# Smaller step intervals for the long convolution (CVL 900 to 760) and for the scan strands (SLG 1.0 to 0.85) in the two hybrid layers of a long fp32 kernel

## The chip, the cores and the metric

The kernel runs on one core of a Trainium2 chip. The metric is the device time of one execution in microseconds. Three executions of the kernel before gave 3419.37, 3421.62 and 3433.52 us; the median, 3421.62 us, is the time that a changed kernel is held against. A further execution was profiled.

## The reference

A model of four layers works on 512 tokens of width 1024 (and in its first two layers on 256 context tokens besides), all in fp32. The first two layers are of another kind and the change does not reach them. The last two are "hybrid" layers, which compute, cut to what matters:

```
proj = h @ w_in                                   # split into q,k,v, z_a, gates of the scan, cf_val, cf_glu, z_b, gate_lg
qkv  = silu(depthwise_conv_centred(qkv, qkv_conv_w))
o    = gated_delta_chunked(q, k, v, g, beta)      # forward, and once more backward in time, 4 heads
y_a  = (rms(o) * dn_norm_w * silu(z_a)) @ w_dn_out
u    = cf_val * sigmoid(cf_glu)                   # 512 channels x 512 tokens
u    = depthwise_conv_centred(u, cf_conv_w) + cf_conv_b      # 31 taps
u    = silu(layer_norm(u, cf_ln_w, cf_ln_b))
y_b  = (u * silu(z_b)) @ w_cf_out
y    = (gate0 * y_a + gate1 * y_b) @ w_out
```

`gated_delta_chunked` takes, for each head and direction, the inverse of a triangular 64x64 matrix per chunk of 64 tokens, and then walks the 8 chunks in order with a state of 128x128.

## The kernel before

**Products.** Each fp32 product is made of three matmuls for each 128 rows of the contraction: activation and weight are split into a high and a low part, and H·wh (L344), L·wh (L347) and H·wl (L348) are summed in PSUM. A product of a full 1024-row contraction is so 8 times 3 = 24 matmuls of 128x512, one with w_cf_out 12. Everything else that TensorE does in a hybrid layer is small: transposes, the inverses and the scans.

**Strands.** `hybrid` (run twice, called hybrid 0 and 1 below) writes its products in this order: gates of the scan, projections of heads 0 and 1, `cf_proj` (8 products, which give the four 128-channel tiles of u), projections of heads 2 and 3, 16 gate products, 4 z_b products ("zb"), then `cf_norm` (the layer norm of the convolution's output), and `branch(1, Yb)`, 8 products of 12 matmuls. Beside them run generators ("strands"): `head(0)`, which does the inverse and scan of head 0 and then of head 2, `head(1)` with heads 1 and 3, and `cf_conv`, the 31-tap convolution, tile by tile: centre tap on ScalarE (L1788), 20 taps on VectorE (L1794, names `cfa<-ld,vecs,cfa`), 10 taps on GpSimd in pairs of a multiply and an add (L1962, L1963), and a VectorE add that joins the two sums (L1967).

**What sets the order.** A planner keeps a clock `now`. After each three matmuls of a product `mmacc` calls `tick`, which adds their planned time and then writes each strand's next step if it is due. A step that yields `(a, b)` adds `a` to the clock and makes the strand due again after `b` x 2.5 x `slow`. Each convolution tap yields `(0, CVL)`, each part of a scan step or of an inverse its own pair, such as `(220, 750)`; `slow` is SLG for both head strands and 1.0 for the convolution. The first TensorE instruction of each step is pinned behind the one that stands ahead of it, so the order on TensorE between products and steps is the planner's. On the other engines a scheduler places the instructions. Where the program needs a strand's end, it calls `wait`, which moves the clock to the earliest due time and writes the steps due then, of all strands, with no product between them. After the last zb product stand these lines:

```
    while any(s[1] is conv for s in K.back):
        K.wait()
    Yb = cf_norm(K, l, zb, U)
```

**cf_norm.** VectorE sums the four tiles, TensorE sums over channels with ones (L1982), the mean is broadcast by a matmul (L388) and subtracted (L1988), the mean square is made in the same way (L374, L364, GpSimd's power L366, L388), and each tile is scaled (L1992), put through Silu (L1993), multiplied with its zb tile (L1994) and split into high and low parts (L324, L325). The first branch product waits for these parts.

**A scan step.** TensorE multiplies with the state (L2124), VectorE makes Pb (L2127), TensorE multiplies with the inverse (L2133), VectorE and ScalarE scale (L2137, L2138), TensorE makes the state's update (L2145), VectorE the state (L2151), TensorE the output (L2157, L2160). An **inverse** is five rounds of a 32-matmul group on a mask of GpSimd's (L739, mask L731), a VectorE transpose (L742) and a ScalarE copy (L743), a second 32-matmul group (L748) and a VectorE subtraction (L749), on which the next L739 waits. L2087, L2088, L2089, L2102 and L2103 prepare it on VectorE.

Of the kernel before, what the change touches and what calls it, by code (L numbers as in the profile page):

```python
# [1756 lines left out]
        K.free(xc[j]["l"], sz[j])  # L1757
    K.free(*ht)

CVL = 900  # L1760
SLG = 1.0
PT = range(1, 31, 3)
HP = 10

# [16 lines left out]
def conv_n(K, dst, src, n, taps, bias=None, skip=()):  # L1781
# [7 lines left out]
    for j in range(len(taps)):  # L1789
# [4 lines left out]
        nc.vector.scalar_tensor_tensor(dst[:, a:b], src[:, a + o:b + o], taps[j], dst[:, a:b], MUL, ADD)  # L1794
        yield 0, CVL


def hybrid(K, CH, l, X):
# [59 lines left out]
    def proj(h):  # L1858
        pre[h] = gdn_proj(K, l, h, X, w)

    def head(a):
        pads = CH.pads(K.p2)
        for h in (a, a + 2):
            while h not in pre:
                yield 0, 2000
            yield from gdn_head(K, CH, l, h, *pre.pop(h), gcT, ngT, beT, bkT, eglT, gcd, egd, Ya, pads)
        K.free(*pads)
# [7 lines left out]
    for h in range(2):  # L1875
        proj(h)
        K.background(heads[h], head(h), slow=SLG)
    cf_proj(K, l, X, w, U)
# [53 lines left out]
def cf_proj(K, l, X, w, U):  # L1932

    nc = K.nc
    for hf in range(2):
        sv = K.wslab(w, 0, KD, 2064 + 256 * hf, 256)
        sg = K.wslab(w, 0, KD, 2576 + 256 * hf, 256)
        for j in range(2):
            pgl = K.gemm_tile(sg[j], X, ONLY_L, range(KD))["l"]
            u = K.p2(name="sgl")  # L1940
            nc.scalar.activation(u, pgl, AF.Sigmoid)
            pvl = K.gemm_tile(sv[j], X, ONLY_L, range(KD))["l"]
            nc.vector.tensor_tensor(u, u, pvl, MUL)
            U[2 * hf + j] = K.out_dram(u, LT)


def cf_conv(K, l, U):

    nc = K.nc
    for t in range(4):  # L1950
# [8 lines left out]
        for j in PT:  # L1959
# [4 lines left out]
            for _ in range(2):  # L1964
                yield next(conv, (0, CVL))
        yield from conv
# [340 lines left out]
```

## Time and profile before

| | |
|---|---|
| median of three runs | 3421.62 us (3419.37 to 3433.52) |
| profiled execution, own time | 3418.44 us |
| its span | 3416.7 us (1.7 us lie around it) |
| TensorE busy (weight loads) | 3151.7 us, 92% (2476.2 us, 72%) |
| VectorE busy | 2122.4 us, 62% |
| ScalarE busy | 1269.4 us, 37% |
| GpSimd busy | 614.0 us, 18% |
| mean granted TensorE clock | 0.953 |

Engine names in rows: PE is TensorE's matmuls, PEld its weight loads, DVE VectorE, ACT ScalarE, POOL GpSimd. L344 is line 344 of the kernel. A timeline row gives start and length in us, engine, line, operation, output and inputs by name, partitions and shape, and the count of records that it sums; in brackets the idle time before it and what ended that. An fp32 matmul outside the products leaves two records, so "x4" there is two instructions. A wait row names who waited for what: microseconds in all, times, the longest. A group row ends with busy time in us and mean ns of one, then the engine's idle time ahead of it. A windows row gives a stretch, its length, the busy time of PE, PEld, DVE, ACT and POOL with the count of instructions, the granted clock (1.00 is 2.4 GHz, 0.50 is 1.2 GHz), the DMA share and GB/s. A branch of the page called the chain follows the work that ended last back to the start.

### The profile page before, as it was taken

What the parts mean: (1) busy time and instruction counts of PE and PEld (TensorE: products, weight loads), DVE (VectorE), ACT (ScalarE), POOL (GpSimd) and SP (SyncE); (2) the same over time, 40 slices, a digit from 0 to 9 for tenths busy, and PEclk for the clock granted to TensorE, in tenths of its full rate; (3) what the DMA queues carried; (4) which work ended last, traced back from release to release, by engine and by line L of the source; (5) the groups of instructions that cost most, each with busy time, mean ns of one, the idle gap of its engine ahead of it and who ended that gap; (6) DMA issues with size and microseconds to landing.
All of it is one profiled execution on the core that took longest, in us unless ns stands there. A gap on an engine that the chain in (4) does not pass through costs nothing.

```text
span 3416.7 us, 61935 instructions
## 1 busy us (share of the span) xinstructions
PE 3151.7 (92%) x25042; PEld 2476.2 (72%) x25042; DVE 2122.4 (62%) x4318; ACT 1269.4 (37%) x2679; POOL 614.0 (18%) x762
## 2 busy tenths in 40 slices
PE   7999898888899999989888999988999899999988
PEld 4878676667688888868765888767667567766756
DVE  4444565645855555685666576677777666677665
ACT  4333343333432222364433332352433335233332
POOL 4111222211000000010010000005156000525500
PEclk8999998999999999999998999989999899999979
DMA  6432554431222222122222223232232343123332
GB/s 228 141 94 70 166 167 155 139 112 52 73 72 68 72 73 97 57 73 69 81 78 82 91 87 132 78 99 78 69 103 95 104 138 102 57 69 108 102 115 90
DMA packets 313570, 336.10 MB, mean 98 GB/s; under 512 B 26542, under 2 KB 259132, under 8 KB 313284
## 3 DMA queue, kind: packets, MB, share of 16 engines
q1 hardware_dynamic: 311172, 329.69, 30.0%
q8 instruction: 197, 3.23, 0.4%
q0 software_dynamic: 2112, 2.45, 0.3%
q14 instruction: 89, 0.73, 0.1%
HBM read 282.13 MB, written 49.94 MB: 97 GB/s over the span
## 4 chain that ended last, share of the span: by engine, by line
PE 61%; issue 18%; DVE 14%; ACT 3%; DMA 3%; POOL 0%; SPq 0%; DVEq 0%; POOLq 0%; ACTq 0%
PE mm L344 14%; PE mm L347 13%; PE mm L348 13%; DVE cfa L1794 3%; PE ps L739 2%; PE ps L748 2%; PE ps L1192 2%; DVE wl L81 2%; PE ps L1137 1%; PE ps L558 1%; PE ps L1719 1%; PE ps L2133 1%; DMA ld<-sp 1%; PE ps L2160 1%; PE ps L1701 1%
## 5 line engine op out<-in xcount | busy, mean ns | idle before, releaser
L344 PE MATMUL mm<-hl,wh 128*128 128x512 f32 (+1 forms) x3296 | 1249.6, 383 | 56.0 <-DVE qkv L1794 15.2
L347 PE MATMUL mm<-hl,wh 128*128 128x512 f32 (+1 forms) x3296 | 1225.8, 372 | 1.6 <-DVE hl L487 1.6
L348 PE MATMUL mm<-hl,wl 128*128 128x512 f32 (+1 forms) x3296 | 1218.5, 372 | 0.0
L344 PEld LDWEIGHTS mm<-hl,wh 128*128 128x128 f32 x3296 | 631.1, 192 | 192.8 <-issue 33.2
L348 PEld LDWEIGHTS mm<-hl,wl 128*128 128x128 f32 x3296 | 631.4, 192 | 114.6 <-issue 2.8
L347 PEld LDWEIGHTS mm<-hl,wh 128*128 128x128 f32 x3296 | 633.2, 192 | 106.3 <-DVE hl L487 3.4
L80 ACT ACTIVATE wh<-wr 128x512 fp32r<-128x512 f32 (+3 forms) x718 | 367.9, 561 | 704.2 <-PE mm L347 614.3
L81 DVE TENSOR_TENSOR wl<-wr,wh 128x512 fp32r<-128x512 f32 (+3 forms) x718 | 435.7, 640 | 230.1 <-ACT wh L80 205.2
L1372 DVE SCALAR_TENSOR_TENSOR cv<-mm,vecs,cv 128x441 f32<-128x441 f32 (+2 forms) x352 | 242.9, 692 | 94.3 <-ACT cv L1360 88.2
L1423 POOL MEMSET gwh<- 128x1024 f32 x3 | 2.9, 955 | 969.2 <-PE mm L347 969.2
L1794 DVE SCALAR_TENSOR_TENSOR cfa<-ld,vecs,cfa 128x497 f32<-128x497 f32 (+14 forms) x160 | 162.1, 1013 | 13.2 <-ACT cfa L1788 11.0
L1962 POOL TENSOR_SCALAR tap<-ld,vecs 128x498 f32<-128x498 f32 (+4 forms) x80 | 150.6, 1882 | 63.9 <-PE ps L2046 29.8
L1395 DVE TENSOR_TENSOR fy<-fy,mm 128x512 f32<-128x512 f32 x96 | 55.2, 577 | 126.3 <-PE mm L348 125.5
L1963 POOL TENSOR_TENSOR cfa<-cfa,tap 128x498 f32<-128x498 f32 (+4 forms) x80 | 112.1, 1401 | 5.3
L743 ACT ACTIVATE pad<-ps 128x256 f32<-128x256 f32 (+1 forms) x100 | 46.7, 468 | 155.5 <-PE ps L739 155.0
L2138 ACT ACTIVATE u<-ps,beT 64x128 f32<-64x128 f32 x128 | 46.2, 362 | 131.3 <-DVE u L2137 130.6
L1374 ACT ACTIVATE cv<-cv,vecs 128x256 f32<-128x256 f32 (+1 forms) x66 | 43.0, 652 | 132.1 <-DVE cv L1372 77.2
L749 DVE TENSOR_TENSOR cut<-cut,ps 128x256 f32<-128x256 f32 x120 | 49.3, 413 | 54.0 <-PE ps L748 53.2
L2137 DVE TENSOR_SCALAR u<-ps,kdT 64x128 f32<-64x128 f32 x128 | 44.5, 349 | 58.4 <-PE ps L2133 44.4
L1378 DVE TENSOR_TENSOR cv<-cv,mm 128x512 f32<-128x512 f32 x66 | 39.5, 599 | 65.5 <-ACT cv L1374 36.2
L425 PE MATMUL ps<-sq,one 128*128 128x512 f32 (+1 forms) x132 | 62.6, 609 | 15.8 <-ACT sq L395 13.7
L731 POOL TENSOR_TENSOR pad<-L,zm 128x512 f32<-128x512 f32 x40 | 54.4, 1360 | 113.4 <-PE ps L739 84.0
(479 smaller groups left out, 4418.9 us busy)
## 6 DMA issues: line engine op xcount, KB each, us to landing
ar<-in_ada_w_dram SPq DMA_DIRECT2D x96, 512.0 KB, 5.2
wr<-in_ffn_up_dram SPq DMA_DIRECT2D x44, 1024.0 KB, 5.0
wr<-in_w_in_dram SPq DMA_DIRECT2D x28, 1024.0 KB, 5.2
ld<-sp SPq DMA_DIRECT2D x84, 256.0 KB, 4.5
wr<-in_w_in_dram SPq DMA_DIRECT2D x32, 512.0 KB, 3.6
xsp<-x SPq DMA_DIRECT2D x48, 256.0 KB, 2.0
x<-xsp SPq DMA_DIRECT2D x48, 256.0 KB, 3.5
wr<-in_ffn_down_dram SPq DMA_DIRECT2D x20, 512.0 KB, 3.7
```

The costliest lines, as they stand in the source:

```text
L80: nc.scalar.activation(h[:, q:e], src, AF.Copy)
L81: nc.vector.tensor_tensor(l[:, q:e], src, h[:, q:e].bitcast(F32), SUB)
L344: mm = nc.tensor.matmul(ps[:m, :n], wh[:, i, :m], H[:, :n], start=first and i == 0, stop=False)
L347: nc.tensor.matmul(ps[:m, :n], wh[:, i, :m], L[:, :n], start=False, stop=False)
L348: nc.tensor.matmul(ps[:m, :n], wl[:, i, :m], H[:, :n], start=False, stop=last and i == nk - 1)
L739: nc.tensor.matmul(ps[r, u * 64:u * 64 + 64], L[r, u], W[r, u], start=True, stop=True)
L748: nc.tensor.matmul(ps[r, u * 64:u * 64 + 64], X[r, u], Z[r, u], start=True, stop=True)
L1192: nc.tensor.matmul(ps[hs[h], d], lhsT(d, h), rhs(d, h), start=first and i == 0 and d == 0, stop=last and i == len(parts) - 1, skip_group_c ...
L1372: nc.vector.scalar_tensor_tensor(t3[:, ro, co], a3[:, ri, ci], tap(ky, kx, ff), t3[:, ro, co], MUL, ADD)
L1794: nc.vector.scalar_tensor_tensor(dst[:, a:b], src[:, a + o:b + o], taps[j], dst[:, a:b], MUL, ADD)
L1962: nc.gpsimd.tensor_scalar(x[:, a:b], src[:, a + o:b + o], taps[j], None, MUL)
L1963: nc.gpsimd.tensor_tensor(g[:, a:b], g[:, a:b], x[:, a:b], ADD)
```

## The change

Two numbers of the planner are smaller; no computation changes.

```
-CVL = 900
-SLG = 1.0
+CVL = 760
+SLG = 0.85
```

CVL stands in `conv_n` (`yield 0, CVL`) and in `cf_conv` (`yield next(conv, (0, CVL))`), SLG in `K.background(heads[h], head(h), slow=SLG)`. In the planner's clock a tap is due 1900 instead of 2250 after the tap before it, and a scan part with `(220, 750)` 1594 instead of 1875.

On TensorE the order at the end of the fourth zb product (`mm_25439`) of a hybrid was this before:

```order
L344 MATMUL mm_25439<-hl_21847,wh_25433 128x512
L347 MATMUL mm_25439<-hl_21848,wh_25433 128x512
L348 MATMUL mm_25439<-hl_21847,wl_25434 128x512
L1982 MATMUL ps_25768<-ones_77,cs_25764 128x1 x4
L2133 MATMUL ps_25493<-Pb_25475,W_24721 64x128
L748 MATMUL ps_25505<-pad_22420,X_24959 64x64
L2133 MATMUL ps_25493<-Pb_25475,W_24721 64x128
L748 MATMUL ps_25505<-pad_22420,X_24959 64x64 x15
L388 MATMUL ps_25775<-ident_72,mu_25773 128x128 x4
L2145 MATMUL ps_25524<-u_4159_25497,kt_24358 128x128
```

From the L1982 row on, 103 small TensorE instructions stand there before the first branch product (71 of the scans, 16 of L748, 16 of `cf_norm`: four each of L1982 and L374, eight of L388). In the changed kernel the same place, the end of the fourth zb product (now `mm_25677`) and the start of the first branch product (`mm_25847`), reads:

```order
L2133 MATMUL ps_25742<-Pb_25722,W_24834 64x128 x2
L388 MATMUL ps_25804<-ident_72,rs_25802 128x128 x4
L2133 MATMUL ps_25751<-Pb_25728,W_24556 64x128
L344 MATMUL mm_25677<-hl_21847,wh_25671 128x512
L347 MATMUL mm_25677<-hl_21848,wh_25671 128x512
L348 MATMUL mm_25677<-hl_21847,wl_25672 128x512
L2133 MATMUL ps_25751<-Pb_25728,W_24556 64x128
L2145 MATMUL ps_25855<-u_4231_25746,kt_24454 128x128
L344 MATMUL mm_25847<-hl_25812,wh_25841 128x512
```

Two small instructions are left between the products; `cf_norm`'s last broadcast (L388 from `rs`) stands ahead of the last three matmuls of the fourth zb product. Its first matmul, L1982, has moved to the end of the first zb product (`mm_25416`):

```order
L344 MATMUL mm_25416<-hl_21841,wh_25410 128x512
L347 MATMUL mm_25416<-hl_21842,wh_25410 128x512
L348 MATMUL mm_25416<-hl_21841,wl_25411 128x512
L2133 MATMUL ps_25446<-Pb_25423,W_24556 64x128
L2145 MATMUL ps_25467<-u_4158_25441,kt_24454 128x128
L2145 MATMUL ps_25468<-u_4158_25441,kt_24454 128x128
L1982 MATMUL ps_25768<-ones_77,cs_25764 128x1 x4
L2145 MATMUL ps_25475<-u_4161_25450,kt_24212 128x128
L2160 MATMUL ps_25484<-u_25440,at_24686 64x128 x2
L388 MATMUL ps_25775<-ident_72,mu_25773 128x128 x4
```

So the convolution's output has to be there some three products earlier in the order than before. On VectorE the convolution's fourth tile (`cfa_25189` in the kernel before) stood around gate products 14 to 16, among these instructions:

```order
L1794 SCALAR_TENSOR_TENSOR cfa_25189<-ld_25187,vecs_21700,cfa_25189 128x509
L749 TENSOR_TENSOR W_24721<-W_24721,ps_24935 128x512
L1794 SCALAR_TENSOR_TENSOR cfa_25189<-ld_25187,vecs_21700,cfa_25189 128x511
L742 STREAM_TRANSPOSE X_24724<-W_24721 128x512
L1794 SCALAR_TENSOR_TENSOR cfa_25189<-ld_25187,vecs_21700,cfa_25189 128x510
L1794 SCALAR_TENSOR_TENSOR cfa_25189<-ld_25187,vecs_21700,cfa_25189 128x509
L81 TENSOR_TENSOR wl_25120<-wr_25116,wh_25119 128x512
```

In the changed kernel (`cfa_25063`) it stands around gate products 9 to 12, together with the preparation of head 3's inverse (`W_24834`) and the rounds of head 2's (`W_24556`):

```order
L2088 TENSOR_TENSOR LT_24687<-E_24508,ps_24677 128x256
L1794 SCALAR_TENSOR_TENSOR cfa_25063<-ld_25061,vecs_21700,cfa_25063 128x503
L2089 TENSOR_TENSOR LT_24687<-LT_24687,beT_21954 128x256 x2
L1794 SCALAR_TENSOR_TENSOR cfa_25063<-ld_25061,vecs_21700,cfa_25063 128x505
L2102 TENSOR_TENSOR W_24834<-LT_24687,zm_15_127 128x512
L749 TENSOR_TENSOR W_24556<-W_24556,ps_24730 128x512
L1794 SCALAR_TENSOR_TENSOR cfa_25063<-ld_25061,vecs_21700,cfa_25063 128x506
```

Before, the preparation of head 3's inverse (L2087 to L2103) stood wholly ahead of this tile's taps, and the taps shared VectorE with the rounds of the two inverses alone; now the preparation stands among them as well.

## Rows read from the trace of the kernel before

**Rows 1.** The page: its span, and the chain that ended last, by engine.

```profile
span 3416.7 us, 61935 instructions
...
PE 61%; issue 18%; DVE 14%; ACT 3%; DMA 3%; POOL 0%; SPq 0%; DVEq 0%; POOLq 0%; ACTq 0%
```

**Rows 2.** Windows by stage: hybrid 0's cf_proj on, gates, zb, gap; last, hybrid 1's gap.

```profile
2307.00:2468.50 161.50, 151.02 (x1353) 115.23 (x1351) 113.42 (x195) 53.85 (x104) 53.98 (x38) 0.98 0.24 76
2468.50:2613.00 144.50, 135.07 (x931) 98.75 (x930) 119.28 (x195) 53.72 (x104) 84.50 (x58) 0.95 0.31 100
2613.00:2649.40 36.40, 35.61 (x440) 28.43 (x437) 17.55 (x29) 10.24 (x21) 30.30 (x21) 1.00 0.23 77
2649.40:2691.10 41.70, 32.07 (x199) 20.41 (x197) 28.16 (x69) 17.06 (x41) 1.04 (x1) 0.63 0.16 51
...
3240.10:3279.80 39.70, 30.68 (x199) 19.55 (x197) 27.99 (x69) 16.64 (x41) 1.04 (x1) 0.59 0.17 54
```

**Rows 3.** Timeline of TensorE from hybrid 0's last zb product to its first branch product.

```profile
2649.40 0.95 PE L1982 MATMUL ps<-ones,cs 128*128 128x1 f32 x8
...
2675.31 0.69 PE L2157 MATMUL ps<-S,qd 128*64 128x128 f32 x4 [2.88 <-DVE S L2151]
...
2691.12 0.79 PE L344 MATMUL mm<-hl,wh 128*128 128x512 f32 x1
```

**Rows 4.** Timeline of TensorE: small instructions between products at the full clock.

```profile
2640.75 1.15 PE L748 MATMUL ps<-pad,X 64*64 64x64 f32 x32
...
2695.09 1.00 PE L2145 MATMUL ps<-u,kt 64*128 64x128 f32 x6
2696.02 0.44 PE L2157 MATMUL ps<-S,qd 128*64 128x128 f32 x4
...
2697.51 0.50 PE L344 MATMUL mm<-hl,wh 128*128 128x512 f32 x1
```

**Rows 5.** Timelines: from cf_norm's last broadcast to a split, hybrid 0, then hybrid 1.

```profile
2663.39 1.11 PE L388 MATMUL ps<-ident,rs 128*128 128x128 f32 x4
...
2671.62 0.69 DVE L325 TENSOR_TENSOR hl<-cfa,hl 128x512 fp32r<-128x512 f32 x1
...
3251.77 1.12 PE L388 MATMUL ps<-ident,rs 128*128 128x128 f32 x4
...
3256.80 0.63 ACT L324 ACTIVATE hl<-cfa 128x512 fp32r<-128x512 f32 x1
...
3258.49 0.68 DVE L325 TENSOR_TENSOR hl<-cfa,hl 128x512 fp32r<-128x512 f32 x1
```

**Rows 6.** Timeline of TensorE behind hybrid 0's last branch(1) products.

```profile
2731.76 0.43 PE L2133 MATMUL ps<-Pb,W 64*64 64x128 f32 x4
...
2736.91 0.49 PE L2145 MATMUL ps<-u,kt 64*128 64x128 f32 x2
```

**Rows 7.** Waits 2329 to 2381, a timeline there, then waits 2577 to 2649.

```profile
PE ps L739 <- DVE W L749: 8.7, 3, 4.4
...
2361.75 5.74 DVE L1794 SCALAR_TENSOR_TENSOR cfa<-ld,vecs,cfa 128x503 f32<-128x503 f32 x5
2370.03 1.97 PE L739 MATMUL ps<-W,pad 64*64 64x64 f32 x32 [4.44 <-DVE W L749]
...
PE ps L739 <- DVE W L749: 1.5, 2, 0.8
```

**Rows 8.** Groups of VectorE: conv taps 2329 to 2366, then 2455 to 2491.

```profile
L1794 DVE SCALAR_TENSOR_TENSOR cfa<-ld,vecs,cfa 128x497 f32<-128x497 f32 (+14 forms) x20 | 23.6, 1182 | 4.8 <-ACT cfa L1788 4.5
...
L1794 DVE SCALAR_TENSOR_TENSOR cfa<-ld,vecs,cfa 128x497 f32<-128x497 f32 (+14 forms) x20 | 19.2, 960 | 0.2
L1794 DVE SCALAR_TENSOR_TENSOR qkv<-mm,vecs,qkv 128x510 f32<-128x510 f32 (+1 forms) x4 | 3.0, 744 | 0.0
```

**Rows 9.** Timeline of GpSimd: first multiply and last add of hybrid 0's fourth tile.

```profile
2605.45 2.09 POOL L1962 TENSOR_SCALAR tap<-ld,vecs 128x498 f32<-128x498 f32 x1 [1.70 <-DMA sp<-gt]
...
2643.14 1.26 POOL L1963 TENSOR_TENSOR cfa<-cfa,tap 128x499 f32<-128x499 f32 x1
```

## The prediction

> **What bounds the kernel now.** I read the page first. Its chain [rows 1] is 61% TensorE and 18% issue (TensorE's own queue moving), so the time is the sum of what TensorE executes and what it waits for; VectorE holds 14% of it. The changed lines act in the two hybrid layers alone, so I went on with windows by stage [rows 2]. The reader should look at the busy column of PE and the clock together. In the products up to the last zb product TensorE is busy 151.0 of 161.5, 135.1 of 144.5 and 35.6 of 36.4 us at clocks of 0.95 to 1.00. The fourth window, behind the last zb product, is another world: 41.7 us, with 32.1 busy at a clock of 0.63, and the same place in hybrid 1 is 39.7 us at 0.59. So I read the timeline of this place [rows 3]: from 2649.40 to 2691.12 no product runs, only small instructions of the scans, the inverses and `cf_norm`, with idle times such as 2.88 us on VectorE's new state. This is the loop that waits for the convolution, then `cf_norm`. Last came the waits and groups in the stages ahead, because work taken out of this gap has to go there [rows 7, 8].
>
> **The gap.** The order of the changed kernel has two small TensorE instructions where 103 stood. What stays is the chain from the fourth zb product to the first branch product. I take it from hybrid 1 [rows 5]: L388 starts at 3251.77, the high part is ready at 3256.80 + 0.63 = 3257.43, 5.7 us later, and the low part at 3258.49 + 0.68 = 3259.17, 7.4 us later. In the new order three matmuls of the last product and two small instructions stand behind that L388, so the last product ends about 1.5 us after L388's start. The first high part then comes 4.2 us after that end, and the wait for the low part adds about 1.5: 5.7, call it 6 us per hybrid. From below, 4.2. From above, 8.9 us, which is this chain in hybrid 0 (2663.39 to 2671.62 + 0.69). Against 41.7 and 39.7 this saves 35.7 + 33.7 = 69.4 us, with +1.8 or -2.9 per hybrid for the bounds.
>
> **What the moved instructions cost among products.** Of 101 that leave the gap in each hybrid, 69 are of the scans, 16 of L748 and 16 of `cf_norm`. Between products at the full clock ten scan instructions (20 records) take 2697.51 - 2695.09 = 2.42 us [rows 4], 0.24 each: 69 x 0.24 = 16.6. Sixteen of L748 take 1.15 us for 32 records: 1.1 with the next one's overlap. `cf_norm`'s sixteen are priced by rows nearby: 0.95 us for four of L1982 [rows 3], as much for four of L374 (same form), and half of 1.12 for each four of L388, since 1.12 was at half the clock [rows 5]: 0.95 x 2 + 0.56 x 2 = 3.0. Sum 20.7, so about 20.6 per hybrid, 41.2 us in all. Bounds: in the same ten, the three of L2145 took 0.93 (0.31 each) and the other seven 1.49 (0.21 each); 69 at 0.21 or 0.31 make it 2 less or 5 more per hybrid. The middle value is the mix, so I keep it.
>
> **The tail.** In the drain behind `branch(1)` the order has nine small instructions fewer: head 3 is one part of a scan step further. That part took 2736.91 - 2731.76 = 5.15 us [rows 6], of which I take 2.8 as the work that now lies ahead among products: -2.3 per hybrid, -4.6.
>
> **Convolution and inverses, denser.** All other steps come sooner too. Nothing is added to any engine; what can change is which tap stands ahead of which inverse step. VectorE has room on average (119.3 of 144.5 us in the gates [rows 2]) but it works in order. The place to read it is the first inverses, which run with the convolution's tile 1: L739 waits 8.7 us there for VectorE's L749, three times, 4.4 at longest, and behind such a wait stand five taps in one piece, 5.74 us, with further work between them and the L749 [rows 7]. In the gates, with tile 4, the same wait is 1.5 us, two times. In the changed order tile 4 stands among head 3's inverse preparation as tile 1 did before, five gate products sooner. I take the middle of 1.5 and 8.7, 5.1: +3.6 per hybrid. A wait also costs clock: a mean of 0.98 over 161.5 us is 3.2 us lost, and if all of it hangs on the 8.7 us, each microsecond of wait costs 1.37. So +5. Tile 2's twenty taps, which spread over 2.7 products, now stand within 1.5, in a stretch with the z_a and q, k, v taps: +1. Each tile's load from DRAM, on SyncE's queue, moves up with its tile; what it costs is seen ahead of tile 1, where VectorE was idle for 4.8 us before the taps, mostly for the centre tap that waits for it [rows 8], and since VectorE then takes up other steps, I cost it at nothing; without that other work it would be those 4.8 us once more for a tile. Together +6 per hybrid, +12. Bounds: none of this, and tile 2 free of GpSimd, where a tap with one input in PSUM took 744 ns against 960 [rows 8]: 20 x 0.216 = -4.3 for a hybrid; or tile 4 wholly like tile 1, 7.2 x 1.37 = 9.9 each, so +20.
>
> **A rule that speaks against it.** Taps take 1182 ns with tile 1, 960 later, and 744 where one input is in PSUM [rows 8]. The Trainium skill, page SBUF — State Buffer, section Who interferes with whom, says that a VectorE instruction with two SBUF inputs and a GpSimd instruction that reads SBUF shut each other out for a whole instruction. The direction of these rows agrees with it. If a denser convolution made all taps of tiles 2 to 4 as long as tile 1's, that were 60 x 0.23 = 14 us of VectorE in each hybrid, 28 us of time if TensorE waited for all of it, and the total would be near 3429. By the rows it is 0, since VectorE has 25 us to spare in the gates alone. I leave it in rival B with a chance of 0.05 within B's.
>
> **Sum.** -69.4 + 41.2 - 4.6 + 12 = -20.8. Against the profiled execution's own 3418.44 (span 3416.7 and 1.7 around it): 3397.6. The median of the runs is 3421.62, 3.2 above that execution; on it the sum gives 3400.8. Between the two I say 3399.
>
> **Rivals.**
> A, the forecast: near 3399.
> B, the denser steps meet the taps: the gap goes, but inverses and scan steps wait more ahead of it, 14 us per hybrid in place of 6. For it: the 4.4 us wait, and taps with 960 ns and more. Against it: TensorE is busy 35.6 of 36.4 us in the zb stage with scans running. 3400.8 + 16 = 3417, no change that can be measured.
> C, slower: TensorE waits at inverse steps while both heads' inverses and tile 4 share VectorE. The price of one wait is 8.7 / 3 = 2.9 us, 4.0 with its clock. Without any new wait a hybrid gains (69.4 - 41.2 + 4.6) / 2 = 16.4; four such waits per hybrid use that up, and above six (16.4 + 8.6 = 25 us) it is slower by over 0.5%. Nine give 2 x (36 - 16.4) = +39, 3460. Against it: an inverse has five rounds, and in tile 1's three waits one alone was over 4 us. A neighbour of it is a late GpSimd: L1982 now stands three products sooner in TensorE's fixed order and needs tile 4's last L1967; the tile took GpSimd 2605.45 to 2643.14 + 1.26, 39 us [rows 9], and in the new order some 5.4 products at about 9 us each lie between its first multiply and its last add, 50 us: 11 us of slack.
> D, cheap: no new waits, tile 2 relieved, the moved instructions at 0.21. 3400.8 - 12 = 3389 without the waits, 3400.8 - 12 - 4 - 8.6 = 3376 with the rest.
> E, the change does not do what it says: VectorE's scheduler places the taps in bursts whatever the interval, the gap is kept in another place, and the time stays at 3421.
>
> **How the numbers follow.** Measured runs here spread so that about 0.5%, 17 us, can be told from no change: faster is below 3404.5, slower above 3438.7. Chances: A 0.47, B 0.27, C 0.08, D 0.15, E 0.03. Faster: D, 0.40 of A and 0.05 of B's better end, 0.60. Same: the rest of A, 0.20 of B, and E, 0.30. Slower: C and 0.02 of B where the rule of the page bites harder than the rows say, 0.10. The range goes from D's lower end, 3376, to the end of B and E, 3421; outside are C, the upper tail of B and a little of D, under 0.2. The likeliest alone is 3390 to 3408: the gap's bounds, the row price's and half of the wait term's.
>
> **What would show it.** In the profile after: the stretch from the last zb product's end to the first branch product is 4 to 9 us instead of 41.7, with no clock of 0.63 in it; the stages from `cf_proj` to the last zb product together grow by about 21 + 6 us in a hybrid (342.5 to some 370 in hybrid 0); L739's waits for L749 at tile 4 are 3 to 8 us; the drain behind `branch(1)` is 2 us shorter. I am wrong if the stages ahead grow by 36 us or more per hybrid, if TensorE stands at L1982 for the convolution, or if scan instructions show waits for VectorE of over 10 us per hybrid ahead of the last zb product.

## The result, and the profile after

The changed kernel takes 3445.18 us (median of six runs, 3436.28 to 3449.45) against 3423.63 us before (six runs, 3419.37 to 3433.52): ratio 1.0058, 95% interval 1.0039 to 1.0077. It is slower by some 20 us, where 3399 was forecast. The profiled execution took 3436.28 us, the fastest of the six, 17.8 us more than the profiled one before. From the page of the changed kernel, the span (before: [rows 1]) and the group of the convolution's taps:

```profile
span 3434.6 us, 61953 instructions
...
L1794 DVE SCALAR_TENSOR_TENSOR cfa<-ld,vecs,cfa 128x497 f32<-128x497 f32 (+14 forms) x160 | 156.1, 979 | 11.3 <-ACT cfa L1788 8.9
```

Next the windows by stage of the changed kernel, answering to [rows 2]: hybrid 0 from `cf_proj` on, gates, zb, gap and branch(1), and last hybrid 1's gap. Columns as there.

```profile
2312.70:2491.10 178.40, 163.31 (x1398) 121.85 (x1398) 126.28 (x227) 56.96 (x115) 69.64 (x49) 0.94 0.23 69
2491.10:2652.20 161.10, 143.33 (x1250) 108.55 (x1249) 116.12 (x178) 54.95 (x106) 100.92 (x67) 0.95 0.30 96
2652.20:2697.40 45.20, 44.05 (x247) 29.42 (x245) 25.30 (x63) 16.75 (x41) 1.04 (x1) 0.96 0.16 48
2697.40:2702.50 5.10, 1.16 (x5) 0.56 (x4) 5.04 (x11) 5.03 (x11) 0.00 (x0) 0.92 0.76 255
2702.50:2747.20 44.70, 42.33 (x215) 27.37 (x216) 27.15 (x74) 13.27 (x39) 1.69 (x2) 0.90 0.47 153
3290.00:3295.20 5.20, 1.35 (x6) 0.72 (x5) 5.14 (x11) 5.10 (x11) 0.00 (x0) 0.71 0.66 227
```

The gap is closed as the change meant: 5.1 and 5.2 us in place of 41.7 and 39.7. But `cf_proj` to the gates grew by 16.9 us, the gates by 16.6 and zb by 8.8. The same stages of hybrid 1, and branch(1) of both hybrids, before:

```profile
2691.10:2730.30 39.20, 38.53 (x204) 25.61 (x204) 22.25 (x63) 11.49 (x36) 0.65 (x1) 0.96 0.47 149
2887.80:3052.00 164.20, 153.95 (x1351) 117.17 (x1349) 112.48 (x195) 53.79 (x105) 53.67 (x38) 0.96 0.24 75
3052.00:3203.30 151.30, 135.23 (x932) 98.44 (x931) 119.89 (x196) 53.68 (x105) 88.92 (x59) 0.95 0.30 96
3203.30:3240.10 36.80, 36.62 (x433) 29.23 (x433) 18.22 (x28) 10.21 (x21) 28.35 (x19) 0.96 0.22 73
3279.80:3320.00 40.20, 38.99 (x203) 25.75 (x203) 22.66 (x64) 11.49 (x36) 0.04 (x1) 0.94 0.48 157
```

and hybrid 1 of the changed kernel:

```profile
2907.10:3085.10 178.00, 162.92 (x1401) 120.82 (x1400) 126.08 (x229) 56.90 (x114) 73.12 (x50) 0.96 0.23 69
3085.10:3246.40 161.30, 143.09 (x1246) 107.93 (x1246) 115.76 (x175) 55.06 (x106) 95.78 (x64) 0.95 0.30 96
3246.40:3290.00 43.60, 42.45 (x247) 28.40 (x245) 25.28 (x63) 16.74 (x40) 1.04 (x1) 1.00 0.18 52
...
3295.20:3340.40 45.20, 42.85 (x215) 27.74 (x216) 27.09 (x74) 13.21 (x39) 1.01 (x1) 0.88 0.48 150
```

These rows allow a split that carries the rest of this text. Of each window, its length less PE's busy time is **idle**; its length times (1 - clock) is what the **lower clock** lost; what is left is **work at the full clock**. For the three stages ahead of the gap together:

| kernel, hybrid | length | idle | lower clock | work |
|---|---|---|---|---|
| before, 0 / 1 | 342.4 / 352.3 | 20.7 / 26.5 | 10.5 / 15.6 | 311 / 310 |
| changed, 0 / 1 | 384.7 / 382.9 | 34.0 / 34.4 | 20.6 / 15.2 | 330 / 333 |

(First row, hybrid 0: idle 161.5 - 151.02 + 144.5 - 135.07 + 36.4 - 35.61 [rows 2]; clock 161.5 x 0.02 + 144.5 x 0.05.) The work grew by 19 and 23 us for some 88 small instructions that now stand there (171 and 178 records more), 0.21 to 0.26 us each. Idle and clock grew by 23.4 and 7.5. The split is good to some 5 us and no better: it charges the clock in idle time too, the same code before lost 10.5 us of clock in one hybrid and 15.6 in the other, and with nearly the same instructions on TensorE later runs of this text give 334, 335 and 338 us of work for the 330 and 333 here. Who waits is in the waits of TensorE, before from 2307 to 2649.4:

```profile
PE ps L739 <- DVE W L749: 10.3, 5, 4.4
PE ps L2157 <- DVE S L2151: 3.4, 6, 1.1
...
PE ps L2124 <- DVE S L2151: 1.8, 3, 1.1
```

and in the changed kernel from 2312.7 to 2697.4:

```profile
PE ps L739 <- DVE W L749: 17.9, 4, 6.9
PE ps L2124 <- DVE S L2151: 6.5, 4, 2.5
PE ps L2157 <- DVE S L2151: 6.1, 8, 1.9
```

Both kinds end on VectorE: the inverses' subtraction (10.3 to 17.9) and the scans' state (5.2 to 12.6). In the gates, where the second inverses run, this stands on VectorE ahead of their first and their fourth L749

```profile
2565.26 5.23 DVE L1794 SCALAR_TENSOR_TENSOR cfa<-ld,vecs,cfa 128x510 f32<-128x510 f32 x4
2570.42 1.69 DVE L81 TENSOR_TENSOR wl<-wr,wh 128x512 fp32r<-128x512 f32 x2
2572.03 5.39 DVE L1794 SCALAR_TENSOR_TENSOR cfa<-ld,vecs,cfa 128x504 f32<-128x504 f32 x6
2577.34 0.67 DVE L749 TENSOR_TENSOR W<-W,ps 128x512 f32<-128x512 f32 x1
...
2605.26 6.92 DVE L1794 SCALAR_TENSOR_TENSOR cfa<-ld,vecs,cfa 128x503 f32<-128x503 f32 x5
2612.10 1.69 DVE L81 TENSOR_TENSOR wl<-wr,wh 128x512 fp32r<-128x512 f32 x2
2613.71 0.67 DVE L749 TENSOR_TENSOR W<-W,ps 128x512 f32<-128x512 f32 x1
```

and this is TensorE there:

```profile
2578.16 1.98 PE L739 MATMUL ps<-W,pad 64*64 64x64 f32 x32 [5.82 <-DVE W L749]
...
2580.66 0.63 PE L347 MATMUL mm<-hl,wh 128*128 128x512 f32 x1
2581.09 0.63 PE L348 MATMUL mm<-hl,wl 128*128 128x512 f32 x1
...
2614.54 3.68 PE L739 MATMUL ps<-W,pad 64*64 64x64 f32 x64 [3.60 <-DVE W L749]
```

These rows show ten taps and two splits ahead of the first L749 (by the order of their widths eight of tile 3's and tile 4's first two), and TensorE waits 5.82 us for it; tile 4's last five and two splits stand ahead of the fourth, 3.60 us. The products behind the first wait start 0.43 us apart, at the lower of the clock's two levels.

The taps themselves are longer in this place. Tiles 3 and 4 of hybrid 0, first before (2527.9 to 2614.6), then in the changed kernel (2537.2 to 2612.2):

```profile
L1794 DVE SCALAR_TENSOR_TENSOR cfa<-ld,vecs,cfa 128x497 f32<-128x497 f32 (+14 forms) x40 | 37.7, 942 | 1.0 <-ACT cfa L1788 0.5
...
L1794 DVE SCALAR_TENSOR_TENSOR cfa<-ld,vecs,cfa 128x497 f32<-128x497 f32 (+14 forms) x40 | 42.3, 1064 | 0.5
```

### The profile page after: what moved, and what is told of

It is laid out like the page before. It is cut to its first block, busy times and chain, and to the rows that moved or that the text cites. A ratio compares the mean times of both kernels' runs of the same rounds, so it can differ in the third digit from the quotient of the medians.

```text
span 3434.6 us, 61953 instructions
## 1 busy us (share of the span) xinstructions
PE 3154.2 (92%) x25042; PEld 2475.2 (72%) x25042; DVE 2118.8 (62%) x4318; ACT 1267.4 (37%) x2679; POOL 614.6 (18%) x762
## 4 chain that ended last, share of the span: by engine, by line
PE 62%; issue 18%; DVE 12%; ACT 3%; DMA 3%; POOL 0%; SPq 0%; DVEq 0%; POOLq 0%; ACTq 0%
PE mm L344 15%; PE mm L347 13%; PE mm L348 13%; PE ps L739 3%; DVE cfa L1794 3%; PE ps L748 2%; PE ps L1192 2%; DVE wl L81 2%; PE ps L1137 1%; PE ps L558 1%; PE ps L1719 1%; PE ps L425 1%; PE ps L2160 1%; DMA ld<-sp 1%; PE ps L2133 1%
## 5 line engine op out<-in xcount | busy, mean ns | idle before, releaser
L344 PE MATMUL mm<-hl,wh 128*128 128x512 f32 (+1 forms) x3296 | 1251.0, 384 | 59.0 <-DVE qkv L1794 15.2
L1794 DVE SCALAR_TENSOR_TENSOR cfa<-ld,vecs,cfa 128x497 f32<-128x497 f32 (+14 forms) x160 | 156.1, 979 | 11.3 <-ACT cfa L1788 8.9
L366 POOL TENSOR_TENSOR rs<-var,mhalf 128x4 f32<-128x4 f32 (+1 forms) x26 | 26.7, 1028 | 347.3 <-DVE var L364 347.2
L2138 ACT ACTIVATE u<-ps,beT 64x128 f32<-64x128 f32 x128 | 46.2, 361 | 110.7 <-DVE u L2137 109.7
L739 PE MATMUL ps<-W,pad 64*64 64x64 f32 x1280 | 52.9, 239 | 36.3 <-DVE W L749 36.3
L749 DVE TENSOR_TENSOR cut<-cut,ps 128x256 f32<-128x256 f32 x120 | 49.2, 412 | 55.1 <-PE ps L748 54.3
L739 PEld LDWEIGHTS ps<-W,pad 64*64 64x64 f32 x1280 | 47.7, 152 | 46.7 <-issue 34.8
```

The costliest lines, as they stand in the source:

```text
L344: mm = nc.tensor.matmul(ps[:m, :n], wh[:, i, :m], H[:, :n], start=first and i == 0, stop=False)
L739: nc.tensor.matmul(ps[r, u * 64:u * 64 + 64], L[r, u], W[r, u], start=True, stop=True)
```

## The experiments

Two theories stood against each other at first. **1a**: the change lost ahead of the gap because TensorE waits behind denser taps on VectorE. **1b**: the gap's instructions cost among products what they cost in it. The time of the kernel before beside each set of runs was 3425.49, 3425.20 and 3428.64 us; ratios are to it.

**One number at a time.** With `CVL = 760` alone:

> The convolution's interval alone is changed (CVL 760, SLG 1.0). Theory 1: the changed kernel is slower because the scans and inverses, made denser, wait for VectorE's taps and cost more among products than in the gap. Here the heads stay as before, so TensorE's waits for L749 ahead of the last zb product stay near 10 to 13 us per hybrid (after the change 18). The gap has 27 small instructions instead of 103 and falls from 41.7 to some 15 us, but 74 scan instructions of each hybrid move into the drain behind branch(1), where no product fills their waits: at the gap's 0.40 us each about 30 us. Sum 2 x (-27 + 30) = +6: 3420 to 3440. Rival: the earlier convolution by itself is what slows the kernel (its taps block VectorE); then the waits for L749 rise to 18 us here too and the time is over 3445.

3434.83 us, ratio 1.0025 (1.0011 to 1.0038), inside the range of the first theory. The gap fell to 7.4 us (some 15 expected) and the drain behind branch(1) rose to 150.6 us in hybrid 0 (119.2 before). The waits for L749 are 14.6 us in hybrid 0 (10 to 13 expected), one of 5.9 at tile 4. In the window from `cf_proj` to the gates TensorE has the same work as before (1351 records, before 1353):

```profile
2310.30:2480.80 170.50, 159.15 (x1351) 120.56 (x1349) 121.96 (x209) 53.31 (x104) 67.34 (x47) 0.93 0.24 72
...
2438.30:2446.30 8.00, 7.28 (x41) 5.10 (x37) 7.55 (x15) 2.56 (x5) 0.00 (x0) 1.00 0.31 97
2446.30:2454.30 8.00, 6.65 (x26) 4.59 (x27) 7.78 (x15) 4.19 (x9) 0.00 (x0) 0.60 0.10 34
```

The same place before, in a window of 8 us:

```profile
2442.00:2450.00 8.00, 7.28 (x49) 4.92 (x48) 4.96 (x13) 4.44 (x10) 1.37 (x2) 1.00 0.01 4
```

Idle is 11.4 us against 10.5, but the clock is 0.93 against 0.98: 9 us longer, nearly all of it clock. The longest wait from 2434 to 2480 is 1.2 us (L2157, for VectorE's state). Hybrid 1 of this run does not repeat it: the same stage took 167.8 us there against 164.2 before, with a clock of 0.95 against 0.96, so 2 us of clock.

With `SLG = 0.85` alone:

> The heads' factor alone is changed (CVL 900, SLG 0.85). Theory 1: the stages up to the last zb product grow as in the changed kernel, by some 38 us per hybrid; the gap keeps 79 small instructions, about 32 us (-9); branch(1) has 6 small instructions instead of 53 (-12) and the drain behind it none of the heads (-8): +9 per hybrid, 3440 to 3445, with waits of about 18 us for L749. Rival: the waits come from the convolution's taps that now stand closer; with CVL 900 they are those of before, 10 to 13 us, and the time is near 3425.

3416.82 us, ratio 0.9971 (0.9962 to 0.9981): faster than both kernels, which neither theory expected. The waits for L749 fell to 7.8 us, below those of before. The stages ahead grew (342.4 to 369.8 us in hybrid 0) and the gap stayed, but the heads are done behind it: from zb's end on, the first two windows of hybrid 0 are

```profile
2676.20:2718.70 42.50, 33.80 (x151) 19.77 (x150) 29.42 (x77) 15.37 (x40) 2.73 (x3) 0.52 0.25 77
2718.70:2744.50 25.80, 25.80 (x107) 20.08 (x106) 13.30 (x33) 8.09 (x24) 1.01 (x1) 0.93 0.66 209
```

with branch(1) at 25.8 us (39.2 before) and the rest up to the next hybrid's projections 106.9 us (119.2 before).

**Without taps.** Both kernels without VectorE's 160 taps, whose steps stay in the planner:

```
-        nc.vector.scalar_tensor_tensor(dst[:, a:b], src[:, a + o:b + o], taps[j], dst[:, a:b], MUL, ADD)
+        len(taps) < 31 and nc.vector.scalar_tensor_tensor(dst[:, a:b], src[:, a + o:b + o], taps[j], dst[:, a:b], MUL, ADD)
```

> The changed kernel without the 20 VectorE taps of each convolution tile (they are left out; the strand's steps, the centre tap and GpSimd's ten taps stay, so the planner's order on TensorE is that of the changed kernel). Read against its partner, the kernel before without the same taps. Theory 1a: what the change lost ahead of the gap is TensorE waiting behind taps on VectorE. Then the waits for L749 fall from 18 us to under 6 us per hybrid, and this kernel is faster than its partner by 5 us or more (+20 for the change as timed, less some 28 for the waits with their clock). Theory 1b: the loss is the price of the moved instructions themselves; then this kernel is slower than its partner by 10 to 20 us, as the changed one is than the one before.

> The kernel before without the 20 VectorE taps of each convolution tile; otherwise the same order on TensorE. The partner of the run ahead of it. Theory 1a: this kernel gains little over before (10 us of waits per hybrid and some clock, 20 to 30 us in all), less than the changed one gains without its taps (40 or more). Theory 1b: both gain the same within 8 us.

3368.31 us (ratio 0.9831, 0.9815 to 0.9848) and 3366.78 us (0.9827, 0.9813 to 0.9842): 1.5 us apart where the whole kernels are 21.6 apart. So the taps cost 57 us before (1a expected 20 to 30) and 77 us after the change, and by the medians most of the slowdown goes with them: 20 us, or 18 give or take 10 by the intervals of the ratios. Waits for L749 are 0.9 us in hybrid 0. The loss hangs on the taps, as 1a has it, but the pair lies between the forecasts of 1a and 1b: the changed kernel did not come out ahead, and closing both gaps was worth nothing even here. The profiled executions show less. From the first tap of q, k, v in hybrid 0 to the end (so that the code which the change does not reach drops out) changed less before is 13.8 us with the taps and 7.0 us without. The windows of the stages ahead, first of the changed kernel without taps (both hybrids),

```profile
2302.70:2659.90 357.20, 349.24 (x2891) 257.34 (x2889) 191.46 (x388) 129.05 (x259) 161.10 (x116) 0.96 0.27 84
...
2867.90:3219.10 351.20, 341.44 (x2891) 251.91 (x2889) 190.72 (x387) 128.84 (x259) 160.43 (x116) 0.99 0.27 86
```

then of the kernel before without them:

```profile
2309.60:2631.40 321.80, 316.66 (x2714) 238.88 (x2713) 173.42 (x337) 118.29 (x229) 161.36 (x116) 0.98 0.29 92
...
2869.00:3188.30 319.30, 314.23 (x2713) 236.75 (x2713) 177.33 (x340) 118.93 (x229) 163.57 (x117) 0.99 0.30 92
```

35.4 and 31.9 us more, of which idle is 2.8 and 4.7 (with taps 13.3 and 7.9); the rest is the instructions and 8 us of clock, nearly all in hybrid 0. The gap gave back 34.5 each.

**Which tile.** The same with the taps of tile 4 alone left out, then with those of tiles 2 and 3:

```
-PT = range(1, 31, 3)
+PT, PT4 = range(1, 31, 3), tuple(range(1, 31, 3))
-        nc.vector.scalar_tensor_tensor(dst[:, a:b], src[:, a + o:b + o], taps[j], dst[:, a:b], MUL, ADD)
+        skip == PT4 or nc.vector.scalar_tensor_tensor(dst[:, a:b], src[:, a + o:b + o], taps[j], dst[:, a:b], MUL, ADD)
-        conv = conv_n(K, U[t], src, LT, taps, K.v(f"cfb{l}", t), PT)
+        conv = conv_n(K, U[t], src, LT, taps, K.v(f"cfb{l}", t), PT4 if t == 3 else PT)
```

(`t in (1, 2)` in the second pair.)

> The changed kernel without the 20 VectorE taps of the fourth convolution tile alone (left out, also in its partner). Theory 1a, narrowed: the loss is tile 4, whose taps now stand among the rounds of the second inverses; TensorE waited there 5.8, 1.6 and 3.6 us for L749. Without them 2 x (11 - 2) us with their clock go, 3445 to 3415 or 3422, and within 6 us of the partner. Rival 1c: the loss is the scans' steps waiting behind taps of tiles 1 to 3 (L2157 and L2124 wait 12 us for the state where they waited 5 to 7 before); then this kernel stays 12 us or more above its partner.

> The kernel before without the 20 VectorE taps of the fourth tile alone. Partner of the run ahead of it. Tile 4 cost TensorE 1.5 us of waits in hybrid 0 and 4.3 in hybrid 1 there, so both theories expect little: 3424 less 6 to 12 us, 3412 to 3418.

> The changed kernel without the 20 VectorE taps of the convolution's second and third tile (left out, in its partner too). Theory 1c: of the 20 us that the change loses through taps, the part that is not tile 4's (about 12) is theirs: in cf_proj and the projections the scans' instructions L2157 and L2124 waited 7.5 us for the state where they waited 1.3 before, and 2.2 with CVL 900 and SLG 0.85. Without these taps the waits fall to 2 or 3 us there, and this kernel stands 7 to 11 us above its partner (tile 4's share), not 21. Rival 1d: what the change loses outside tile 4 is a matter of the granted clock and of the moved instructions and hangs on no tile; then it stands 15 to 22 us above its partner.

> The kernel before without the 20 VectorE taps of the second and third tile. Partner of the run ahead of it. Its scans hardly waited for these taps (1.3 us ahead of the gates, 5 us among them): 5 to 20 us below the kernel before under both theories.

Tile 4 out: 3428.54 (1.0010, 1.0001 to 1.0020) against 3414.66 (0.9968, 0.9956 to 0.9980), 13.9 us apart. Tiles 2 and 3 out: 3402.37 (0.9922, 0.9905 to 0.9938) against 3389.28 (0.9887, 0.9872 to 0.9902), 13.1 apart. The first falls to 1c, not to "tile 4 alone"; the second lies between 1c and 1d. The kernel before gained 39 us without tiles 2 and 3, where 5 to 20 were expected. Of some 20 us about 8 hang on tile 4, 8 on tiles 2 and 3, and what is left, 4, on tile 1, if shares add up; by the intervals each is uncertain by about 8 us, so no share is shown by itself, only that no one tile holds the whole. Without tiles 2 and 3 the changed kernel's waits for the state ahead of the gates fell from 7.5 to 0.7 us, as 1c has it. In the changed kernel without tile 4's taps the gates' and zb's waits of L739 are still

```profile
PE ps L739 <- DVE W L749: 5.9, 1, 5.9
```

against 11.0 with them: that is the wait behind tile 3's last taps.

**Denser, and at the old pace.** `CVL = 650` with the rest as changed:

> The changed kernel with a still denser convolution, CVL 650 in place of 760 (SLG 0.85). On TensorE the order is almost that of the changed kernel, two instructions in the gap. On VectorE tile 4's taps come before most of the second inverses: ahead of their second to fourth L749 stand 3, 0 and 2 instructions of taps and splits in place of 2, 3 and 7. Theory 1a: it is the place of the taps, not how dense they are, that costs: the third wait (3.6 us) and the second go, 4 to 6 us per hybrid with clock, 3430 to 3437. Rival: a denser convolution waits more everywhere: 3450 or more.

3446.29 us, ratio 1.0063 (1.0045 to 1.0080), no better, and in neither of the two expected ranges. The waits for L749 at the gates and zb fell from 11.0 to 6.5 us as the order let expect, but ahead of them the clock fell: `cf_proj` to the gates of hybrid 0 took

```profile
2306.10:2494.60 188.50, 170.77 (x1401) 125.95 (x1400) 132.46 (x230) 56.91 (x114) 85.77 (x57) 0.91 0.22 66
```

which is 10 us more than with 760. What the order saved at the second inverses went again ahead of the gates.

Then the convolution at its old pace, heads as changed, and a loop that writes the convolution alone:

```
-CVL = 760
+CVL = 900
-    while any(s[1] is conv for s in K.back):
-        K.wait()
+    for s in [s for s in K.back if s[1] is conv]:
+        while s in K.back: K.step(s)
```

> CVL 900 as before, SLG 0.85 as changed, and the loop behind the last zb product writes the remaining steps of the convolution alone, not those of the heads. So the gap is short (11 small instructions) and the heads' steps stand in branch(1) and the drain as in the changed kernel, but the convolution keeps its old pace. Theory 1a: stages ahead of the gap like those with SLG alone (370 to 375 us per hybrid, waits of 21 us), gap 5 to 10 us, branch(1) 45 us: faster than both kernels, 3408 to 3420. Rival 1b: filling the gap costs what it saves whatever the taps do, since its instructions then run among products; then it is no faster than the kernel before, 3424 or more.

3421.26 us, ratio 0.9983 (0.9970 to 0.9996). Stage windows of hybrid 0:

```profile
2307.70:2479.90 172.20, 161.38 (x1401) 120.18 (x1400) 120.88 (x220) 56.80 (x115) 62.27 (x43) 0.96 0.23 71
2479.90:2628.50 148.60, 140.51 (x1245) 106.14 (x1244) 113.27 (x186) 55.55 (x106) 85.04 (x56) 0.98 0.33 104
2628.50:2672.90 44.40, 41.65 (x235) 27.20 (x233) 21.15 (x54) 14.58 (x36) 25.54 (x17) 1.00 0.20 62
2672.90:2687.10 14.20, 5.01 (x19) 3.68 (x18) 9.82 (x21) 7.59 (x16) 1.04 (x1) 0.61 0.16 51
2687.10:2733.50 46.40, 43.66 (x213) 28.17 (x214) 27.10 (x72) 13.18 (x38) 1.70 (x2) 0.86 0.47 147
```

Idle ahead of the gap is 21.7 us and clock 9.9, as before (20.7 and 10.5), with 334 us of work: in this run the denser heads bring no more waits and no fall of the clock. The 160 taps took 144.8 us of VectorE, 905 ns each, against 156.1 and 979 with 760. So in this order, on TensorE nearly that of the changed kernel, CVL's step from 900 to 760 is worth -9 us in each gap and +19.5 in the stages ahead in hybrid 0, +24 us in the medians. And 1b is nearly right of what remains: 27 us of gap saved in hybrid 0, some 23 of work added ahead and 7 in branch(1). At 4 us below the kernel before it missed the range of 1a by 1 us and that of 1b by 3, and its interval overlaps that of SLG alone.

**Denser heads.** The same loop with `SLG = 0.70`:

> CVL 900, SLG 0.70, and the loop behind the last zb product writes the convolution's steps alone. The heads end before branch(1) does, so that nothing of theirs is left in the drain (none of 15 instructions), and 18 small instructions stand in the gap. If moving the heads' work among products is worth what it saves in a drain (about 13 us per hybrid less there with SLG 0.85 alone) and the taps keep their pace, 3400 to 3415. If the heads' steps, denser still, run into the taps (ahead of the fifth L749 of the first inverses 7 taps and splits now stand), 3420 or more.

3486.86 us, ratio 1.0172 (1.0153 to 1.0190). The gates of hybrid 0 went to 179.0 us at 0.91 with waits of 5.5 us on the state, 4.2 on u and 3.9 on the head's output, and the drain did not shrink (129.8 us to the next projections): the range of the second expectation, and far into it, but by the scans' waits: those for L749 are 1.7 us there.

## Why the prediction was wrong, point by point

Against the profiled executions the terms stand so, forecast then measured:

- **Gap**, -69.4: -71.1 (41.7 to 5.1, 39.7 to 5.2). Right in size. The longest wait in it was not drawn: 3.58 us for the scan's scale L2138, which stands on ScalarE behind the four Silu of `cf_norm`; the waits for the split are 0.38 and 0.59 us (rows of ScalarE, then of TensorE):

```profile
2698.62 2.55 ACT L1993 ACTIVATE cfa<-cfa,vecs 128x512 f32<-128x512 f32 x4
2701.07 0.74 ACT L2138 ACTIVATE u<-ps,beT 64x128 f32<-64x128 f32 x2
...
2701.47 0.67 PE L2145 MATMUL ps<-u,kt 64*128 64x128 f32 x2 [3.58 <-ACT u L2138]
2702.52 0.79 PE L344 MATMUL mm<-hl,wh 128*128 128x512 f32 x1 [0.38 <-ACT hl L324]
2703.90 0.80 PE L347 MATMUL mm<-hl,wh 128*128 128x512 f32 x1 [0.59 <-DVE hl L325]
```

- **Moved instructions**, +41.2: 48. In the stages ahead 19 and 23 us, ahead of `cf_proj` 1.6 and 2.8 (20 records more stand there), in branch(1) about 1 each. The price from [rows 4] was about right.
- **Tail**, -4.6: -2.8.
- **Convolution and inverses, denser**, +12: about 40. This is the step that failed. Idle ahead of the gap rose by 13.3 and 7.9 us where 4.6 each were taken, the lower clock by 10.1 and -0.4. And branch(1), to which no wait was charged, lost 1.7 and 1.1 more in idle (0.59 of each is the wait for the low part, which the prediction counted in the gap) and 2.9 and 3.0 in clock, since it starts at a clock that the short gap leaves low (0.90 and 0.88 against 0.96 and 0.94).

The sum is +14; the other 4 us of the two spans lie ahead of the first hybrid, with no difference in the code: its first tap of q, k, v starts at 2256.5 us before and at 2260.6 after, and anywhere from 2250.6 to 2262.3 in the profiles of this study. In the medians the loss is 21.6.

Inside the failed step "the middle of 1.5 and 8.7", 5.1 us, was right for tile 4 itself: 11.0 less the 5.8 behind tile 3's end. What was missing is three other things. Tile 3's end now stands among the second inverses too, 5.8 us. The scans were left out of the sum although their chain runs through VectorE at every step: their waits on the state rose by 7.4 us in hybrid 0. And the clock was charged by the microsecond of wait (1.37 with the wait), and none in branch(1); the stretch with CVL alone shows 9 us of clock in hybrid 0 and 2 in hybrid 1 for about one microsecond more of idle each, so the clock has no such price here. Two of the prediction's own signs of being wrong came: the stages ahead grew by 42.3 us in hybrid 0 (30.6 in hybrid 1; the mark was 36), and the scans waited 12.6 and 12.1 us for VectorE (the mark was 10). VectorE's spare time "on average" did not help, since it works in order: the stage has room, the place ahead of one L749 has none.

Rival C named the place, the second inverses, and a break-even of four waits of 2.9 us per hybrid; hybrid 0 had 11.0 us in three such waits, against 1.5 before, with the scans' waits on top. Rival B had the mechanism with 14 us per hybrid; it measured about 20, so the time ended beyond B's range. The length of the taps, which B also named, is not cleared: the 160 took 156.1 us in all after the change and 162.1 before, but those of tiles 3 and 4, behind which the second inverses wait, went from 942 to 1064 ns, and with the same heads the old pace has 144.8 us. The Trainium skill, page SBUF — State Buffer, section Who interferes with whom, says that a VectorE instruction with two SBUF inputs and a GpSimd instruction that reads SBUF shut each other out. The trace agrees: in hybrid 0, from a tile's first to its last tap, GpSimd was busy for 21.9 us with tile 2 before and 0.5 after, for 25.1 and 36.5 with tile 3, and the taps grew shorter and longer with it. No run separates the length of the taps from their place. D had tile 2 right (its taps fell from 960 to 739 ns in hybrid 0) and the waits wrong; E fell, since the gap closed.

Shown by runs: the loss goes with the taps (with and without them) and with their pace (900 against 760 with the same heads, 24 us in the medians; 650 costs no more than 760), and it comes with longer waits on L749 and L2151. How it divides between place, length and clock stays open. That the clock falls because of these waits is not shown, and one pair speaks against it as the whole: without the taps, and nearly without these waits, the stages ahead still lost 8 us more of clock after the change than before (17.8 against 9.6 over both hybrids, by the windows above), where the kernels with taps differ by 9.7.

## What to carry to other kernels

A stall with work in it is not worth its length: here closing it gave back 36.6 us, and its instructions cost some 24 us elsewhere, so 13 at most were to be had, and they go again if the filled-in work waits. Before making steps denser, list for each in-order engine what will stand directly ahead of the instruction that the bottleneck waits for, in the new order, not the engine's mean share. Change one pacing number at a time: of this pair, the heads' alone made the kernel 0.3% faster, and the convolution's alone slower.

## What the runs showed of the hardware that was not expected

The granted clock fell where TensorE had hardly waited. With CVL alone it was 0.60, 0.76 and on for 32 us in hybrid 0, in a stretch whose longest wait was 1.2 us, while the kernel before held 1.00 there; that stage lost 9 us, and 2 in hybrid 1. In the changed kernel without taps it fell from 1.00 to 0.70 with still less idle time ahead of it:

```profile
2438.00:2446.00 8.00, 7.92 (x46) 5.45 (x44) 6.37 (x14) 3.43 (x8) 1.01 (x1) 1.00 0.00 0
2446.00:2454.00 8.00, 7.85 (x41) 5.61 (x41) 2.94 (x10) 1.67 (x4) 5.34 (x5) 0.70 0.00 0
```

The Trainium skill, page TensorE: Matmul & The Clock Gate, section HAM oscillation, describes the loss for long waits on transfers. No such wait stands in these rows. What stands ahead of the fall is a piece of small instructions alone: from 2446.1 to 2450.7 TensorE ran 32 records of the scans and of a norm back to back, and the products behind them start 0.43 us apart in place of 0.23. With CVL alone such a piece stands there too, from 2444.5 to 2450.1, with two waits of 0.8 and 1.2 us in it. Whether the small instructions or the waits bring the clock down no run separates.
